# Scores in a bank pool of six, masks moved from TensorE to VectorE, and weights of two query blocks transposed in one visit

## The chip, the cores and the metric

The kernel runs on one core of one Trainium2 chip. The metric is the device time of one execution in microseconds (us). TensorE does matmuls and transposes into PSUM (eight banks of 128 partitions x 512 fp32), VectorE and ScalarE read these banks, POOL (GpSimd) works on SBUF alone, and SP (SyncE) issues most DMAs.

## The reference

One layer of a streaming encoder for 1024 prompt frames and 64 sample frames of width 1024, all in fp32:

```
h = rmsnorm(x)
q_a,k_a,v_a | q_b,k_b,v_b | f_b | gate = h @ W_in          # 8 heads of 64 in each branch, q and k normed
A: chunk-band attention: a frame reads its chunk of 64 and the 8 chunks before, bias by relative distance
B: forgetting attention: causal softmax, logit[t,s] += c[t] - c[s], c = cumsum(log sigmoid(f))
x = x + (sigmoid(gate_a) * (A @ W_pa) + sigmoid(gate_b) * (B @ W_pb)) @ W_o
x = x + HierMoE(rmsnorm(x))                                # top-1 of 4 groups, top-2 of its 8 experts
```

It returns the new x of both parts and the new key, value and forget-gate caches.

## The kernel before

**Precision.** Each fp32 operand is split into a high and a low part in the faster fp32r type; a product is two or three matmuls. So nearly every result that TensorE leaves in PSUM is read twice: ScalarE writes the rounded high part, and VectorE subtracts it from the result to get the low part.

**Stages.** First come eight passes `qkv(x)`, one for each pair of heads (four pairs of the band attention, four of the forgetting one). A pass goes through nine tiles of frames; each is a group of 24 matmuls of 384 columns (16 for the last kind of tile) into one `big` bank, which ScalarE copies to `raw` (L380). The attention of pair x runs beside the pass of pair x+1, in between its matmuls. Then come the gates, the sample frames' attention beside them, the merges with `w_pa` and `w_pb`, the output product with routing, and 32 experts, whose weights are loaded as buffers come free.

**Order.** TensorE's instructions keep the order in which the program writes them. ScalarE's, VectorE's and POOL's order is set by the compiler's own simulation as it schedules. Each `tick` in a projection (one for three matmuls) runs what is due: `at(dt, ...)` counts ticks, and `late(dt, ...)` counts `clock`, the kernel's own sum of matmul and transpose times in us. Scores of a query block come every 4.5 ticks (`PACE`). The constants are `D_W0` (8) from scores to the first part of the weights, `D_W1` (1.2) from there to the second part, `D_VAL` (4.5) to the values, and `D_TURN` (10) from the norm of q and k to their transposes.

**One head of one group.** The 1024 query frames are four groups g of two blocks j of 128. For a head and a block, `scores` multiplies q by up to 8 key blocks (5 in the band), in one or two pieces of up to 512 columns; each piece goes to a `big` bank. VectorE adds the bias and takes the row minimum (L598). In the forgetting branch VectorE has before that written bias minus c into S (L585), and TensorE adds a causal mask to the last 128 columns by a matmul of an identity with `tribig`. `softmax` takes the exponential on ScalarE (L536), the reciprocal on VectorE (L538), and scales S on ScalarE (L540). `weights` transposes S on TensorE, up to four 128x128 blocks to a `small` bank, for each block j and each part on its own; ScalarE copies the high part to `PT` (L635), and VectorE makes the low one (L636). `values` multiplies v by `PT` for both blocks.

**q and k.** `normalize` squares and sums the rows of two tiles (ScalarE L405, VectorE L408 and L410), POOL takes the power (L411) and scales the rows (L422), and `turn_qk` transposes them into another `small` bank. `stack_q` (L495) makes high and low parts of q for each group, the low ones in two buffers by turns.

**PSUM.** One pool `pp` has four `big` banks (projections, scores, gates, merges, output, experts' second products) and four `small` ones (all transposes, values, and others).

Of the kernel before, what the change touches and what calls it, by code (L numbers as in the profile page):

```python
# [24 lines left out]
CAP = 96  # L25
NOV = 22
EPS = 1e-6
NBIG, NSMALL = 4, 4
O_TURN, O_LOG, O_RANK, O_TAB = 3, 4, 7, 3
SA, SB, PTA, PTB, NORM_POOL, D_NORM, ATT0, ATT1, WPOOL, WR, SS, WO_EVERY, PF, SQ, FOX_POOL, V_POOL, RC_ACT, KT, NX, NN, NU0, E0, YB = 4, 3, 2, 1, 2, 0, 2, 26, 0, 4, 1, 3.5, 3, 2, 0, 2, 2, 1, 10, 1, 8, -1, 3  # L30
# [5 lines left out]
NW, FPAIR, D_TURN, H_NORM, H_TURN, GRP = 16, 1, 10, 0, 4, 2  # L36
D_W0, D_W1, D_VAL, PACE = 8, 1.2, 4.5, 4.5
# [9 lines left out]
class K:  # L47
    def __init__(self, tc, I, O):
        self.tc, self.nc, self.I, self.O = tc, tc.nc, I, O
        self.t, self.seq, self.due, self.later, self.clock = 0, 0, [], [], 0.0  # L50
# [136 lines left out]
    def turn_h(self, i, k0):  # L187
        nc, x, n = self.nc, self.xs[i], rows(i)
        ps = self.pp.tile([128, 4, 128], F32, name="small", bufs=NSMALL)
# [74 lines left out]
    def forget(self):  # L264
# [45 lines left out]
        def sums():  # L310
            pc = self.pp.tile([128, 2, 104], F32, name="small", bufs=NSMALL)
# [14 lines left out]
        def store():  # L326
            pn = self.pp.tile([104, 128], F32, name="small", bufs=NSMALL)
# [86 lines left out]
    def normalize2(self, br, p, i0, c, raw, T, r):  # L414
# [36 lines left out]
        self.late(D_TURN, self.turn_qk, br, p, i0, c, raw, T)  # L451

    def turn_qk(self, br, p, i0, c, raw, T):
# [3 lines left out]
        pt = self.pp.tile([128, 2, 2, 128], F32, name="small", bufs=NSMALL)  # L457
# [112 lines left out]
    def scores(self, br, p, g, h, j, T, bias, G, H):  # L570
# [13 lines left out]
        if br == 1:  # L584
            (nc.gpsimd if FOX_POOL else nc.vector).tensor_scalar(  # L585
                S[:, :n], bias[h][:, :n], self.cc[:, i, 2 * p + h:2 * p + h + 1], None, op0=OP.subtract)
        pcs = self.pieces(n)
        for x, (o, m) in enumerate(pcs):
            ps = self.pp.tile([128, 512], F32, name="big", bufs=NBIG)
            ks = slice(128 * kb0 + o, 128 * kb0 + o + m)  # L590
            qs = slice(128 * j, 128 * j + 128)
            last = br == 1 and x == len(pcs) - 1
# [10 lines left out]
        self.late(D_W0, self.weights, br, p, g, h, j, T, G, H, 0)  # L603

    def weights(self, br, p, g, h, j, T, G, H, u):

        nc = self.nc
        b0, nb = self.blocks(br, g)
        i = 2 * g + j
        kb0 = max(0, i - 4) if br == 0 else 0  # L610
        if u == 0:
            if nb > 4:
                self.late(D_W1, self.weights, br, p, g, h, j, T, G, H, 1)
        if j == 1 and u == (nb > 4):
            self.late(D_VAL, self.values, br, p, g, h, T, G, H)
        if ("PT", u) not in H:
            m, bufs = (2, self.pt_bufs) if u == 1 and nb == 6 else (4, 2)
            PT = H["PT", u] = self.ap_.tile([128, 2, m, 256], F32R, name=f"PT{m}", bufs=bufs)
            for b, jj in ((2 * g + 1, 0), (b0, 1)) if br == 0 and g >= 2 else ((2 * g + 1, 0),):
                uu, r = divmod(b - b0, 4)  # L620
                if uu == u:
                    nc.gpsimd.memset(PT[:, :, r, 128 * jj:128 * jj + 128].bitcast(F32), 0.0)
        PT = H["PT", u]
        r0, r1 = kb0 - b0, i - b0
        a, b = max(r0, 4 * u), min(r1, 4 * u + 3)
        if a > b:
            return
        S = H["S", j]
        pt = self.pp.tile([128, 4, 128], F32, name="small", bufs=NSMALL)
        for r in range(a, b + 1):  # L630
            c = (r - r0) * 128
            self.tr(pt[:, r - 4 * u, :], S[:, c:c + 128], self.ident)
        sr = slice(a - 4 * u, b + 1 - 4 * u)
        hi = PT[:, 0, sr, 128 * j:128 * j + 128]
        nc.scalar.copy(hi, pt[:, sr, :])  # L635
        nc.vector.tensor_tensor(PT[:, 1, sr, 128 * j:128 * j + 128], pt[:, sr, :], hi.bitcast(F32), op=OP.subtract)  # L636

    def values(self, br, p, g, h, T, G, H):
# [4 lines left out]
        po = self.pp.tile([128, 256], F32, name="small", bufs=NSMALL)  # L643
        for r in range(nb):
            u, rr = divmod(r, 4)
            for hl in range(2):
                self.mm(po, T["v"][(b0 + r) // 4][:, (b0 + r) % 4, h, :], H["PT", u][:, hl, rr, :],
# [23 lines left out]
    def sample2(self, br, p, P, rk, rv, qk, qh, ql):  # L671
        nc, I = self.nc, self.I
        pt = self.pp.tile([128, 4, 128], F32, name="small", bufs=NSMALL)
# [7 lines left out]
        def head(h):  # L681
# [15 lines left out]
            if br == 1:  # L697
                nc.vector.tensor_scalar(S, bias[:, :576], self.cc[:64, 12, hd:hd + 1], None, op0=OP.subtract)
            for x, o in enumerate((0, 288)):
                ps = self.pp.tile([128, 512], F32, name="big", bufs=NBIG)  # L700
                sl = slice(o, o + 288)
                last = br == 1 and x == 1
                self.mm(ps[:64, :288], qh[:, h], ks[h][:, sl], start=True, stop=False)
                self.mm(ps[:64, :288], ql[:, h], ks[h][:, sl], start=False, stop=not last)
                if last:
                    self.mm(ps[:64, 224:288], self.identb[:64, :64], self.tribig[:64, :64],
                                     start=False, stop=True)
# [7 lines left out]
        def weights(h, V, S):  # L715
            pt = self.pp.tile([128, 5, 64], F32, name="small", bufs=NSMALL)
# [11 lines left out]
        def values(h, V, PT):  # L728
            rw = slice(64 * h, 64 * h + 64)
            po = self.pp.tile([128, 256], F32, name="small", bufs=NSMALL)  # L730
# [125 lines left out]
    def out(self, m0):  # L856
# [9 lines left out]
        self.ptab = self.pp.tile([CAP, 3, 32], F32, name="ptab", tag="big", bufs=NBIG)  # L866
# [33 lines left out]
    def out_tile(self, i, mh, ml):  # L900
# [5 lines left out]
        def turn(k0):  # L906
            pt = self.pp.tile([128, 4, 128], F32, name="small", bufs=NSMALL)
# [29 lines left out]
        def logits():  # L937
            pl = self.pp.tile([128, 40], F32, name="small", bufs=NSMALL)
# [68 lines left out]
    def place(self, i, n, OH, E):  # L1007
# [3 lines left out]
        pp = self.pp.tile([128, 32], F32, name="small", bufs=NSMALL)  # L1011
# [59 lines left out]
    def turn(self, xg):  # L1071
# [3 lines left out]
        for k0 in (0, 4):  # L1075
            pt = self.pp.tile([128, 4, CAP], F32, name="small", bufs=NSMALL)
# [5 lines left out]
    def hidden(self, u, xT):  # L1082
        nc = self.nc
        ph = self.pp.tile([128, 2, CAP], F32, name="small", bufs=NSMALL)
# [74 lines left out]
    def overflow(self):  # L1159
# [8 lines left out]
        pc = self.pp.tile([128, 32], F32, name="small", bufs=NSMALL)  # L1168
# [70 lines left out]
    def run(self):  # L1239
# [24 lines left out]
        self.pp = self.open("pp", 1, PSUM)  # L1264
        pairs = [(br, p) for br in range(2) for p in range(4)]
# [152 lines left out]
```

## Time and profile before

| | |
|---|---|
| median of 3 runs | 1245.71 us (1242.77 to 1245.74) |
| profiled execution: its time, its span | 1241.81 us, 1240.0 us |
| busy in the span: TensorE, its weight loads | 96%, 89% |
| VectorE, ScalarE, POOL | 64%, 60%, 25% |
| granted TensorE clock, mean | 0.985 |

A group of instructions in the profile stands as line, engine, operation, output<-inputs by the program's names, shape and count, then its busy time and the mean duration of one in ns, then the idle time of its engine just before it with what ended that. PE is TensorE's matmuls (transposes among them), PEld its weight loads, DVE is VectorE and ACT is ScalarE. Matmuls are pipelined: the start of one to the start of the next tells what it costs, and the duration shown is longer.

### The profile page before, as it was taken

How to read it: one execution, taken by the hardware profiler on the slowest of the kernel's cores; microseconds unless marked ns; L12 is line 12 of the kernel's file. 1: busy time of each engine (PE TensorE's matmuls, PEld its weight loads, DVE VectorE, ACT ScalarE, POOL GpSimd, SP SyncE). 2: the span in 40 equal slices, each digit the busy share in tenths (PEclk: the TensorE clock that was granted, in tenths of full speed). 3: DMA queues.
4: the chain of work that ended last, by engine and by line, in shares of the span. 5: the costliest groups of instructions: out<-in, count | busy, mean ns of one | idle time of the engine just before them, and what ended most of it. 6: DMA issues, size and time to landing. Idle time of an engine off the chain costs nothing. (4 is left out here: it accounts for less than half of the span.)

```text
span 1240.0 us, 22375 instructions
## 1 busy us (share of the span) xinstructions
PE 1190.5 (96%) x7677; PEld 1105.5 (89%) x7677; DVE 788.6 (64%) x2412; ACT 740.9 (60%) x1730; POOL 314.9 (25%) x469
## 2 busy tenths in 40 slices
PE   8999999999999999999999999999999989999993
PEld 6999999999889999899899889999988859999983
DVE  5667776767388887967467686318644444666543
ACT  5789998989498898988566443423233322333331
POOL 2643435352433434100000000000000013445421
PEclk9999999999999999999999999999999998999988
DMA  8112121222322131411233332214584458999995
GB/s 283 50 61 80 44 73 52 71 65 71 69 66 73 53 84 35 81 53 32 73 92 116 104 91 75 88 33 132 199 292 161 159 195 251 302 288 285 287 290 137
DMA packets 102538, 156.31 MB, mean 126 GB/s; under 512 B 13581, under 2 KB 77941, under 8 KB 102389
## 3 DMA queue, kind: packets, MB, share of 16 engines
q1 hardware_dynamic: 92789, 124.43, 32.6%
q0 software_dynamic: 7168, 21.50, 8.1%
q10 hardware_dynamic: 2464, 8.91, 1.9%
q8 instruction: 61, 1.00, 0.3%
q14 instruction: 56, 0.46, 0.1%
HBM read 122.08 MB, written 38.23 MB: 129 GB/s over the span
## 5 line engine op out<-in xcount | busy, mean ns | idle before, releaser
L83 PE MATMUL big<-w,hTh 128*128 128x384 f32 (+1 forms) x1152 | 324.3, 354 | 1.6 <-ACT hTh L193 0.7
L83 PEld LDWEIGHTS big<-w,hTh 128*128 128x128 f32 x1152 | 204.6, 189 | 6.2 <-DVE w L234 1.0
L83 PE MATMUL big<-hTh,w 128*128 128x384 f32 (+1 forms) x768 | 205.7, 336 | 0.0
L83 PE MATMUL big<-w,hTl 128*128 128x384 f32 (+1 forms) x512 | 173.6, 339 | 0.9 <-DVE hTl L194 0.9
L83 PEld LDWEIGHTS big<-hTh,w 128*128 128x128 f32 x768 | 138.6, 189 | 1.2
L83 PE MATMUL big<-hTl,w 128*128 128x384 f32 (+1 forms) x384 | 126.4, 329 | 0.0
L636 DVE TENSOR_TENSOR PT<-small,PT 128x512 fp32r<-128x512 f32 (+2 forms) x192 | 98.9, 520 | 21.1 <-ACT PT L635 19.2
L536 ACT ACTIVATE S<-S,mns 128x640 f32<-128x640 f32 (+7 forms) x128 | 94.3, 737 | 26.3 <-DVE mns L598 25.3
L83 PE MATMUL big<-ath,w 128*128 128x384 f32 (+1 forms) x384 | 99.4, 335 | 0.0
L540 ACT ACTIVATE S<-S,rc 128x640 f32<-128x640 f32 (+7 forms) x128 | 94.0, 736 | 7.8 <-DVE rc L538 6.9
L83 PEld LDWEIGHTS big<-w,hTl 128*128 128x128 f32 x512 | 97.0, 190 | 1.3 <-DVE hTl L194 1.2
L95 PE MATMUL small<-ident,S 128*128 128x128 f32 x528 | 89.3, 273 | 4.7 <-ACT S L540 2.6
L635 ACT CAST PT<-small 128x512 fp32r<-128x512 f32 (+2 forms) x192 | 85.1, 448 | 11.3 <-PE small L95 6.7
L83 PE MATMUL small<-PT,v 128*128 128x256 f32 x608 | 83.5, 283 | 0.0
L411 POOL TENSOR_TENSOR ssr<-ssa,mhalf 128x8 f32<-128x8 f32 (+1 forms) x40 | 61.2, 1531 | 72.6 <-DVE ssa L410 55.9
L83 PEld LDWEIGHTS small<-PT,v 128*128 128x128 f32 x608 | 79.3, 188 | 0.1
L83 PE MATMUL big<-wo,mh 128*128 128x512 f32 x288 | 75.9, 402 | 0.0
L95 PEld LDWEIGHTS small<-ident,S 128*128 128x128 f32 x528 | 65.0, 140 | 10.2 <-ACT S L540 3.8
L83 PEld LDWEIGHTS big<-hTl,w 128*128 128x128 f32 x384 | 72.9, 190 | 0.0
L83 PEld LDWEIGHTS big<-ath,w 128*128 128x128 f32 x384 | 69.0, 190 | 1.4
L83 PE MATMUL big<-k,qh 128*128 128x320 f32 (+3 forms) x192 | 64.4, 339 | 3.2 <-DVE mns L598 3.2
L449 POOL TENSOR_TENSOR v<-raw,v 128x128 fp32r<-128x128 f32 x64 | 31.2, 487 | 133.3 <-DVE v L448 125.9
(259 smaller groups left out, 2568.9 us busy)
## 6 DMA issues: line engine op xcount, KB each, us to landing
uo<-in_w SPq DMA_DIRECT2D x43, 512.0 KB
ux<-in_w SPq DMA_DIRECT2D x30, 512.0 KB
ur<-in_w SPq DMA_DIRECT2D x23, 512.0 KB
wraw<-in_w_pair SPq DMA_DIRECT2D x56, 192.0 KB
wraw<-in_w_in SPq DMA_DIRECT2D x32, 192.0 KB
atd<-at SPq DMA_DIRECT2D x32, 128.0 KB
bias<-ccd SPq DMA_DIRECT2D x8, 512.0 KB
y<-in_x_prompt SPq DMA_DIRECT2D x8, 512.0 KB
```

The source lines that it names most:

```text
L83: self.nc.tensor.matmul(out, a, b, start=start, stop=stop)
L95: self.nc.tensor.transpose(out, a, ident)
L411: nc.gpsimd.tensor_tensor(r[:n, :4 * c], a[:n, :4 * c], self.mhalf[:n, :4 * c], op=OP.pow)
L449: (nc.gpsimd if V_POOL & 2 else nc.vector).tensor_tensor(V[:, i, :, 64:128], src, V[:, i, :, 0:64].bitcast(F32), op=OP.subtract)
L536: nc.scalar.activation(S[:nq, :n], S[:nq, :n], AF.Exp, bias=mn[:nq], scale=-1.0, accum_out=sm[:nq])
L540: nc.scalar.activation(S[:nq, :n], S[:nq, :n], AF.Copy, scale=rc[:nq])
L635: nc.scalar.copy(hi, pt[:, sr, :])
L636: nc.vector.tensor_tensor(PT[:, 1, sr, 128 * j:128 * j + 128], pt[:, sr, :], hi.bitcast(F32), op=OP.subtract)
```

## The change

- The banks: two `big` ones for projections and all that came after them, six `small` ones in a pool of their own, `ps`. The scores of prompt and samples go to `small`. Ahead of the output product `ps` is closed and opened again with one bank for the table of places and five `small` ones.
- The mask matmuls go, in prompt and samples. In place of the one L585 over n columns VectorE does n - 128 columns as before, and the last 128 in a scalar_tensor_tensor that subtracts c and adds `tribig`.
- `RC_ACT` 2 to 1: S of block j = 1 is scaled on VectorE, that of j = 0 still on ScalarE.
- `weights` runs once for a head and group, 7 units of `clock` after the scores of j = 1, and does all pieces of both blocks in a row; five blocks are cut 3 + 2 and six 3 + 3, where they were cut at four. `PT` is one tile for all key blocks: two buffers in the band, one in the forgetting branch.
- The transposes of q and k are put on a list 5 units after their norm begins. The next `weights` does all that stands there at its end; what has not been done 9 units after the norm began is done then.
- S has four buffers in the forgetting branch, not three, and the low part of q there one, not two.

The diff at its core:

```
-NBIG, NSMALL = 4, 4
+NBIG, NSMALL = 2, 6
-SA, SB, ..., FOX_POOL, V_POOL, RC_ACT, ... = 4, 3, ..., 0, 2, 2, ...
+SA, SB, ..., V_POOL, RC_ACT, ... = 4, 4, ..., 2, 1, ...
-NW, FPAIR, D_TURN, H_NORM, H_TURN, GRP = 16, 1, 10, 0, 4, 2
-D_W0, D_W1, D_VAL, PACE = 8, 1.2, 4.5, 4.5
+NW, FPAIR, D_TURN, D_TURN2, H_NORM, H_TURN, GRP = 16, 1, 5, 9, 0, 4, 2
+D_W0, D_VAL, PACE = 7, 4.5, 4.5
...
+    def turned_tile(self, k):
+
+        return self.ps_.tile([128, 4, 128], F32, name="small", bufs=NSMALL)[:, :k]
...
-        self.late(D_TURN, self.turn_qk, br, p, i0, c, raw, T)
+        x = [self.turn_qk, br, p, i0, c, raw, T]
+        self.late(D_TURN, lambda: self.turns.append(x))
+        self.late(D_TURN2, self.turn_now, x)
+
+    def turn_now(self, *which):
+
+        for x in which or tuple(self.turns):
+            if any(x is y for y in self.turns):
+                self.turns = [y for y in self.turns if y is not x]
+                x[0](*x[1:])
...
-        self.q_lows(self.ap_, 256, 2)
+        self.q_lows(self.ap_, 256, 2 - br)
...
-            (nc.gpsimd if FOX_POOL else nc.vector).tensor_scalar(
-                S[:, :n], bias[h][:, :n], self.cc[:, i, 2 * p + h:2 * p + h + 1], None, op0=OP.subtract)
+            c = self.cc[:, i, 2 * p + h:2 * p + h + 1]
+            if i:
+                nc.vector.tensor_scalar(S[:, :n - 128], bias[h][:, :n - 128], c, None, op0=OP.subtract)
+            nc.vector.scalar_tensor_tensor(S[:, n - 128:n], bias[h][:, n - 128:n], c, self.tribig,
+                                           op0=OP.subtract, op1=OP.add)
...
-            ps = self.pp.tile([128, 512], F32, name="big", bufs=NBIG)
+            ps = self.ps_.tile([128, 512], F32, name="small", bufs=NSMALL)
...
-            self.mm(ps[:, :m], ql[:, h, qs], K[:, ks], start=False, stop=not last)
-            if last:
-                self.mm(ps[:, m - 128:m], self.identb, self.tribig, start=False, stop=True)
+            self.mm(ps[:, :m], ql[:, h, qs], K[:, ks], start=False, stop=True)
...
-        self.late(D_W0, self.weights, br, p, g, h, j, T, G, H, 0)
+        if j == 1:
+            self.late(D_W0, self.weights, br, p, g, h, T, G, H)
...
+        self.late(D_VAL, self.values, br, p, g, h, T, G, H)
+        PT = H["PT"] = self.ap_.tile([128, 2, self.wide // 128 + 1 - br, 256], F32R, name="PT", bufs=self.pt_bufs)
+        for b, jj in ((2 * g + 1, 0), (b0, 1)) if br == 0 and g >= 2 else ((2 * g + 1, 0),):
+            nc.gpsimd.memset(PT[:, :, b - b0, 128 * jj:128 * jj + 128].bitcast(F32), 0.0)
+        for j in range(2):
+            i = 2 * g + j
+            kb0 = max(0, i - 4) if br == 0 else 0
+            r0, n = kb0 - b0, i + 1 - kb0
+            S = H["S", j]
+            m = -(-n // -(-n // 4))
+            for a in range(0, n, m):
+                b = min(a + m, n)
+                pt = self.turned_tile(b - a)
+                for r in range(a, b):
+                    self.tr(pt[:, r - a, :], S[:, 128 * r:128 * r + 128], self.ident)
+                hi, lo = (PT[:, x, r0 + a:r0 + b, 128 * j:128 * j + 128] for x in range(2))
+                nc.scalar.copy(hi, pt)
+                nc.vector.tensor_tensor(lo, pt, hi.bitcast(F32), op=OP.subtract)
+        self.turn_now()
```

## Rows read from the trace of the kernel before

**Rows 1.** The page, part 1: busy us, share of the span, instructions.
```profile
PE 1190.5 (96%) x7677; PEld 1105.5 (89%) x7677; DVE 788.6 (64%) x2412; ACT 740.9 (60%) x1730; POOL 314.9 (25%) x469
```

**Rows 2.** Busy time by stretch: us, engines in order, PEclk, DMA share, GB/s.
```profile
310.00:392.00 82.00, 77.24 (x490) 70.84 (x488) 58.12 (x165) 61.97 (x143) 34.35 (x55) 1.00 0.30 73
```

**Rows 3.** Waits of PE, 60 to 610: total us, times, longest.
```profile
PE big L83 <- DVE mns L598: 3.2, 4, 1.8
PE small L95 <- ACT S L540: 2.6, 3, 1.8
```

**Rows 4.** Timeline of PE, 411 to 416: start, us, instruction, count.
```profile
411.10 0.27 PE L95 MATMUL small<-ident,S 128*128 128x128 f32 x1
411.13 0.42 PE L83 MATMUL big<-w,hTh 128*128 128x384 f32 x1
411.39 0.34 PE L83 MATMUL big<-w,hTl 128*128 128x384 f32 x1
...
411.75 0.60 PE L95 MATMUL small<-ident,raw 128*128 128x128 f32 x4
412.11 0.78 PE L83 MATMUL big<-w,hTh 128*128 128x384 f32 x3
...
415.70 0.23 PE L83 MATMUL big<-tribig,identb 128*128 128x128 bf16 x1
415.74 1.48 PE L83 MATMUL big<-w,hTh 128*128 128x384 f32 x7
```

**Rows 5.** Groups of DVE by form, 60 to 610: busy us, mean ns.
```profile
L213 DVE SCALAR_TENSOR_TENSOR w<-wraw,small,w 128x128 fp32r<-128x128 f32 x62 | 19.0, 347 | 4.0 <-ACT w L212 3.7
...
L585 DVE TENSOR_SCALAR S<-bias,cc 128x1024 f32<-128x1024 f32 x8 | 6.2, 769 | 0.4 <-PE small L95 0.4
...
L585 DVE TENSOR_SCALAR S<-bias,cc 128x768 f32<-128x768 f32 x8 | 4.9, 613 | 0.9 <-PE small L95 0.9
```

**Rows 6.** By stretch: third, fourth groups of the first three forgetting pairs; 391.90: second pair's first two.
```profile
351.60:371.70 20.10, 18.36 (x121) 16.56 (x120) 19.06 (x54) 19.76 (x47) 5.49 (x9) 1.00 0.29 88
371.70:391.90 20.20, 19.92 (x130) 18.02 (x128) 18.14 (x48) 18.85 (x37) 9.76 (x15) 1.00 0.35 91
391.90:421.30 29.40, 29.40 (x198) 27.93 (x198) 20.43 (x61) 23.50 (x58) 10.67 (x18) 1.00 0.11 31
421.30:440.10 18.80, 17.78 (x119) 16.74 (x118) 18.15 (x52) 18.21 (x42) 4.13 (x7) 1.00 0.39 115
440.10:459.70 19.60, 19.60 (x130) 17.93 (x129) 16.69 (x45) 17.97 (x36) 9.53 (x15) 1.00 0.33 62
488.90:509.40 20.50, 18.29 (x120) 16.95 (x119) 19.20 (x64) 20.00 (x53) 3.84 (x8) 1.00 0.29 87
509.40:528.20 18.80, 18.80 (x131) 17.50 (x130) 17.15 (x47) 18.45 (x41) 5.26 (x8) 1.00 0.45 67
```

**Rows 7.** Timeline around the forgetting attention's start.
```profile
321.23 0.34 SPq L652 DMA_DIRECT2D atd<-at  x1
321.61 1.11 SPq L527 DMA_DIRECT2D bias<-ccd  x2
...
330.45 0.55 DVE L585 TENSOR_SCALAR S<-bias,cc 128x128 f32<-128x128 f32 x2 [4.40 <-DMA bias<-ccd]
```

**Rows 8.** Timeline: POOL scales q and k, TensorE transposes them.
```profile
193.75 1.19 POOL L422 TENSOR_TENSOR raw<-raw,ssr 128x256 f32<-128x256 f32 x2
...
195.45 0.60 PE L95 MATMUL small<-ident,raw 128*128 128x128 f32 x4
...
443.71 1.66 POOL L422 TENSOR_TENSOR raw<-raw,ssr 128x256 f32<-128x256 f32 x2
...
446.85 0.61 PE L95 MATMUL small<-ident,raw 128*128 128x128 f32 x4
```

**Rows 9.** Timeline in the second merge.
```profile
869.86 0.31 PE L83 MATMUL big<-atl,w 128*128 128x320 f32 x1
...
870.15 0.55 DVE L775 SCALAR_TENSOR_TENSOR z<-z,big 128x384 f32<-128x384 f32 x1
```

More of the change, by code (lines that the diff above doesn't have):

```diff
@@ L49, in __init__ @@
         self.tc, self.nc, self.I, self.O = tc, tc.nc, I, O
+        self.turns = []
         self.t, self.seq, self.due, self.later, self.clock = 0, 0, [], [], 0.0
@@ L188, in turn_h @@
         nc, x, n = self.nc, self.xs[i], rows(i)
-        ps = self.pp.tile([128, 4, 128], F32, name="small", bufs=NSMALL)
+        ps = self.turned_tile(4)
         for k in range(4):
@@ L310, in sums @@
         def sums():
-            pc = self.pp.tile([128, 2, 104], F32, name="small", bufs=NSMALL)
+            pc = self.turned_tile(2)[:, :, :104]
             lff = lf.rearrange("p i h -> p (i h)")
@@ L326, in store @@
         def store():
-            pn = self.pp.tile([104, 128], F32, name="small", bufs=NSMALL)
+            pn = self.turned_tile(1)[:104, 0]
             self.tr(pn, ccf, self.ident)
@@ L602, in scores, with weights @@
         self.softmax(mns[:, x:x + 1], S, n, 128, j < RC_ACT)
-        self.late(D_W0, self.weights, br, p, g, h, j, T, G, H, 0)
-    def weights(self, br, p, g, h, j, T, G, H, u):
+        if j == 1:
+            self.late(D_W0, self.weights, br, p, g, h, T, G, H)
+    def weights(self, br, p, g, h, T, G, H):
         nc = self.nc
         b0, nb = self.blocks(br, g)
[L609 to L636, printed above, removed]
@@ L672, in sample2 @@
         nc, I = self.nc, self.I
[L673 removed]
+        pt = self.ps_.tile([128, 4, 128], F32, name="small", bufs=NSMALL)
         for i in range(4):
@@ L697, in head @@
             if br == 1:
-                nc.vector.tensor_scalar(S, bias[:, :576], self.cc[:64, 12, hd:hd + 1], None, op0=OP.subtract)
+                c = self.cc[:64, 12, hd:hd + 1]
+                nc.vector.tensor_scalar(S[:, :512], bias[:, :512], c, None, op0=OP.subtract)
+                nc.vector.scalar_tensor_tensor(S[:, 512:], bias[:, 512:576], c, self.tribig[:64, :64],
+                                               op0=OP.subtract, op1=OP.add)
             for x, o in enumerate((0, 288)):
-                ps = self.pp.tile([128, 512], F32, name="big", bufs=NBIG)
+                ps = self.ps_.tile([128, 512], F32, name="small", bufs=NSMALL)
                 sl = slice(o, o + 288)
-                last = br == 1 and x == 1
                 self.mm(ps[:64, :288], qh[:, h], ks[h][:, sl], start=True, stop=False)
[L704 to L707, printed above, removed]
+                self.mm(ps[:64, :288], ql[:, h], ks[h][:, sl], start=False, stop=True)
                 add = bias[:, sl] if br == 0 else S[:, sl]
@@ L865, in out @@
         self.free = deque("x" * NX)
-        self.ptab = self.pp.tile([CAP, 3, 32], F32, name="ptab", tag="big", bufs=NBIG)
+        self.close("ps")
+        self.ps_ = self.open("ps", 1, PSUM)
+        self.ptab = self.ps_.tile([CAP, 3, 32], F32, name="ptab", bufs=1)
         self.next_e, self.ew, self.which = 0, [], []
@@ L937, in logits @@
         def logits():
-            pl = self.pp.tile([128, 40], F32, name="small", bufs=NSMALL)
+            pl = self.ps_.tile([128, 40], F32, name="small", bufs=NSMALL - 1)
             for k in range(8):
@@ L1010, in place @@
         V = nc.vector
-        pp = self.pp.tile([128, 32], F32, name="small", bufs=NSMALL)
+        pp = self.ps_.tile([128, 32], F32, name="small", bufs=NSMALL - 1)
         for j in range(2):
@@ L1083, in hidden @@
         nc = self.nc
-        ph = self.pp.tile([128, 2, CAP], F32, name="small", bufs=NSMALL)
+        ph = self.ps_.tile([128, 2, CAP], F32, name="small", bufs=NSMALL - 1)
         for j in range(2):
@@ L1167, in overflow @@
         self.placed = None
-        pc = self.pp.tile([128, 32], F32, name="small", bufs=NSMALL)
+        pc = self.ps_.tile([128, 32], F32, name="small", bufs=NSMALL - 1)
         for j in range(2):
```

19 lines of the change are left out of this document (9 added, 10 removed).

## The prediction, made before the result was known

> **What bounds the kernel now.** I began with the page's shares of the span: TensorE is busy for 96% of it [rows 1], so the first question is whether a matmul goes, or a wait of TensorE. The table by stretches shows where its waits lie: in the 82 us around the start of the forgetting attention TensorE is busy for 77.24 us, at a granted clock of 1.00, and the slow clock is no part of this story [rows 2]. The list of waits adds what ended them: 3.2 us for the row minimum of line 598 and 2.6 us for the scaled weights of line 540, the two largest of some 10 us between 60 and 610 us [rows 3]. So in the eight pairs of heads TensorE's own instructions set the time, save in a few places where VectorE or ScalarE comes late. Behind them gates, merges, the output product and the experts follow in TensorE's written order; a microsecond won or lost in the pairs moves all of that, the experts' weight loads too, since these start as buffers come free. The sum therefore holds terms of the pairs and few others.
>
> **Gathering the transposes.** In the timeline of TensorE, the matmul behind one transpose starts 0.03 us after it, and takes 0.42 us in place of the 0.34 of the matmul after it: 0.11 us in all. Four in a row start at 411.75 and the next matmul at 412.11, with the same lengthening behind it: 0.36 + 0.08 = 0.44 us, again 0.11 each [rows 4]. So a visit to the transposes costs nothing beyond its transposes, and gathering five visits into one gains 0 us. The bound on either side is the reading error of such a row, 0.01 us on some 100 visits: 1 us.
>
> **The masks.** 64 matmuls against `tribig` in the prompt and 8 in the samples go. The one at 415.70 lets the projections start after 0.04 us; seven of these then take 1.48 us, where 0.34 + 6 x 0.175 = 1.39 would be usual, so 0.13 us in all [rows 4]. I take 0.10, since some of the lengthening would stand behind the scores alone as well; bounds 0.04 and 0.13. All 72 are worth 7.2 us (2.9 to 9.4). By the Trainium skill (TensorE: Matmul & The Clock Gate, Back-to-back issue gap) a stream of 128-column matmuls runs at about 81 ns each; that estimate would make it 72 x 0.081 = 5.8 us.
>
> **What VectorE takes over.** Two things come to it. The j = 1 half of the scalings, which the trace shows on ScalarE only: as a tensor_scalar from SBUF to SBUF it is like line 585, 0.613 us at 768 columns and 0.769 at 1024. And the mask: line 585 gets 128 columns shorter, (0.769 - 0.613) / 2 = 0.08 us, and a scalar_tensor_tensor of 128 columns is added, like line 213 with 0.347 us: +0.27 us [rows 5]. A forgetting group of queries has two heads and two blocks. Its third group gains 2 x 0.613 + 4 x 0.27 = 2.31 us, its fourth 2 x 0.769 + 4 x 0.27 = 2.62 us.
>
> Is there room? In the table by groups, VectorE idles in the third groups of the first three pairs for 1.04, 0.65 and 1.30 us, in the fourth for 2.06, 2.91 and 1.65 [rows 6]. What doesn't fit: 1.27 + 1.66 + 1.01 in the third, 0.56 + 0 + 0.97 in the fourth, 5.5 us in all, and I take that as added time. It can be 0, if the backlog runs on into the emptier first groups, or 3 x (2.31 + 2.62) = 14.8 us, if none of the idle can be used since VectorE waits there for ScalarE. With these six groups bound by VectorE, the 24 masks in them save nothing: 48 x 0.10 = 4.8 us are left of the 7.2. In first and second groups, busy for 20.43 of 29.40 us in the second pair [rows 6], the added work costs 0, and so I count it for the fourth pair, which has no next pair's weights to split, and for the band attention, whose VectorE is in none of the larger waits; if that cover went, 32 scalings of the band at some 0.6 us would be 19 us, and I hold that for out of reach.
>
> **ScalarE's relief** is 64 scalings. It holds no one up but in the 2.6 us of [rows 3]: gain 1.5 us, bounds 0 and 2.6.
>
> **The start of the forgetting attention.** The bias load at 321.61 us is issued behind the last store of the band attention, and VectorE begins line 585 at 330.45 after 4.40 us of idle [rows 7]. The last weights come 8 + 1.2 units after their scores now, 7 then; a unit is a microsecond of the kernel's own count (0.160 us for a 384-column matmul, which takes about 0.18 by [rows 4]), so all behind them, the load too, comes 2.2 x 1.1 = 2.4 us sooner. TensorE loses 4.8 us in that stretch [rows 2]; I take 2.4 us back, bounds 0 and 4.8. The scores no longer share banks with the projections there.
>
> **q and k turned earlier.** Now 10 units after the norm begins, then at the end of a visit between 5 and 9, or at 9. The row that is turned must be normalized by POOL first. For the last tiles of a pair that ends at 445.37, and the transposes start at 446.85, 1.5 us later; in the band attention 194.94 and 195.45, 0.5 us [rows 8]. One unit earlier eats the second slack and most of the first. A visit that falls at 5 to 6 units, 4.5 x 1.1 = 5 us sooner, would leave TensorE waiting 3.5 us or more; behind it wait all projections. ScalarE's relief shortens the same chain, whose first steps are its copy and square. I take +1.5 us; bounds 0 and 9 (six pairs at 1.5).
>
> **Values behind larger visits.** They still come 4.5 units after the visit begins, but four pieces, up to 15 transposes of 0.11 us, are now inside that time, and ScalarE's and VectorE's copies of the pieces come at once. I take +1.0, bounds 0 and 4 (eight visits with 15 transposes, at 0.5 us).
>
> **One low part of q** is left in the forgetting attention. The next group's must wait till the last scores of this one are done, and the next scores come 4.5 ticks, 13.5 matmuls or some 2.4 us, later; two VectorE instructions, by line 213 some 0.4 us each (an estimate), must fit in, and TensorE's scores and projections are queued behind them. Cost 0; bound 5 (twelve changes of group at 0.4 us). The fourth S buffer can only take waits away. POOL's zeroing of the one PT tile waits for the values before, which come some 3 us ahead of the next visit: 0.
>
> **Two banks for the projections.** In the pairs and gates a group of 24 matmuls lasts 4.2 us and the copy behind it is done sooner, cost 0. In the second merge a group has 12 matmuls, 2.1 us, and VectorE lags: the third group of an output column starts about 869.7, while VectorE takes the first one's result from 870.15 to 870.70 [rows 9]. With two banks it must wait, 1.0 us; the lag doesn't add up from group to group, as TensorE's wait lets VectorE catch up. +0.7, bounds 0 and 1.5. The experts keep the order of their loads; cost 0.
>
> **Sum**, against the profiled execution's 1241.81 us: -4.8 +5.5 -1.5 -2.4 +1.5 +1.0 +0.7 = 0.0 us, 1241.8. The profiled execution lies 3.9 us under the median of the runs shown, 1245.71; moved there, 1245.7. What a measurement of this kernel can tell from no change is about 0.3%, 3.7 us.
>
> **Rivals.**
> 1. *The cover holds* (faster). VectorE's backlog is carried into the emptier first groups, and the turns and values find their data ready: -7.2 - 1.5 - 2.4 + 0.7 = -10.4, 1235.3 us. For it: the first two groups of the next pair, on which the full ones border, leave VectorE 9 us idle [rows 6]. Against it: the queue of TensorE is in order, so a late score stops the projections behind it.
> 2. *VectorE becomes the bound of the forgetting attention* (slower). Mechanism: third and fourth groups of the first three pairs; price: all 14.8 us as added time, since VectorE's idle there is waiting that no reordering fills: -4.8 + 14.8 - 1.5 - 2.4 + 1.5 + 1.0 + 0.7 = +9.3, 1255.0 us. It decides from where VectorE's added work in a group exceeds its idle in it, which is so in five of the six. The Trainium skill (Perfetto Trace Analysis, Optimization Strategy) says that a gap repeating on the engine that should be saturated can mean too few buffers. As a mechanism of this kernel: scores, turned weights and values now go round six banks, some ten per head, and each is held till VectorE has read it; if VectorE lags, TensorE waits for a bank. No run here shows that, and the time would be that of this rival.
> 3. *The turns come too early* (slower): 9 in place of 1.5 in the sum: +7.5, 1253.2 us. For it, the 0.5 us of slack in [rows 8]; against it, ScalarE's relief in just this chain.
> 4. *The turns keep their own time*: few visits fall between 5 and 9 units, so the q and k are turned alone, one unit earlier. The change then doesn't do what it says; as visits cost nothing, the time is that of the forecast.
>
> **Chances.** Forecast with rival 4: 0.36. Rival 1: 0.33. Rivals 2 and 3: 0.20 and 0.11. The forecast's own range is 1242 to 1249. For 8 in 10 the range must reach to the first two rivals: 1233 to 1257. Faster by over 0.3%: 0.33; within it: 0.36; slower: 0.31.
>
> **What would show it.** Right: the `tribig` matmuls gone and no shorter visits otherwise; VectorE over 97% in third groups of the first three pairs, with TensorE's waits there of some 2 us a pair; line 585's first start after the band's last store some 2.4 us sooner; ScalarE under 90% in these groups. Wrong: TensorE without waits from 390 to 530 us (rival 1), waits for line 598 or the weights' copies of over 10 us in sum there (rival 2), waits of the turns for POOL's normalized rows in most pairs (rival 3). A change of the stretches behind 620 us by over 3 us would mean that I missed a part.

## The result, and the profile after

The changed kernel takes 1257.23 us (median of 4 runs, 1252.58 to 1258.61) where the kernel before took 1244.24 in the runs beside it: a ratio of 1.0101, with a 95% interval of 1.0066 to 1.0136. It is slower. The forecast was no change, and the time lies 0.2 us above the range.

Its profiled execution has a span of 1256.0 us, 16.0 more than before. Line numbers move: L422 is now L427, L585 is L601 with the mask in L602, L598 is L612, L540 is L554 on ScalarE and L556 on VectorE, L636 is L641, L380 is L385; matmuls stand in L84 (before L83), transposes in L100 (before L95). The two profiled executions lie further apart than the medians (16.2 us, not 13.0). First the page's busy times of the kernel after, against [rows 1].

```profile
PE 1186.8 (94%) x7605; PEld 1110.0 (88%) x7605; DVE 828.4 (66%) x2540; ACT 697.3 (56%) x1666; POOL 313.2 (25%) x467
```

TensorE has 72 instructions and 3.7 us of work fewer, and yet the span grew: the loss is time in which TensorE does nothing. The next view lists what TensorE waited for in the kernel after, 60 to 630 us (total us, times, longest), the counterpart of [rows 3].

```profile
PE small L100 <- POOL raw L427: 10.7, 14, 2.4
PE small L100 <- DVE S L556: 3.1, 3, 1.7
PE small L84 <- DVE PT L641: 2.5, 6, 0.7
PE big L84 <- ACT raw L385: 2.4, 1, 2.4
PE small L84 <- DVE mns L612: 1.4, 2, 0.7
```

The largest line is new: the transposes of q and k wait for POOL's scaled rows. Its 14 waits belong to 7 of the 40 turns: a turn of two tiles waits once for each tile's product. In the timeline of the kernel after (start, us, engine, what; in brackets the idle time before and what ended it) one such wait stands first, and then the start of the forgetting attention.

```profile
128.45 1.67 POOL L416 TENSOR_TENSOR ssr<-ssa,mhalf 128x8 f32<-128x8 f32 x1 [1.78 <-DVE v L453]
...
130.08 0.46 POOL L454 TENSOR_TENSOR v<-raw,v 128x128 fp32r<-128x128 f32 x1
...
130.49 1.19 POOL L427 TENSOR_TENSOR raw<-raw,ssr 128x256 f32<-128x256 f32 x2
...
131.17 0.33 PE L100 MATMUL small<-ident,raw 128*128 128x128 f32 x1 [2.44 <-POOL raw L427]
...
131.74 0.90 PE L100 MATMUL small<-ident,raw 128*128 128x128 f32 x3 [0.24 <-POOL raw L427]
...
329.52 0.34 SPq L657 DMA_DIRECT2D atd<-at  x1
...
329.95 1.10 SPq L541 DMA_DIRECT2D bias<-ccd  x2
...
338.82 0.35 DVE L602 SCALAR_TENSOR_TENSOR S<-bias,cc,tribig 128x128 f32<-128x128 f32 x1 [8.04 <-DMA bias<-ccd]
...
342.39 0.35 DVE L602 SCALAR_TENSOR_TENSOR S<-bias,cc,tribig 128x128 f32<-128x128 f32 x1 [2.42 <-DMA bias<-ccd]
...
343.12 0.15 DVE L552 RECIPROCAL rc<-sm 128x1 f32<-128x1 f32 x1
...
343.31 0.40 ACT L554 ACTIVATE S<-S,rc 128x128 f32<-128x128 f32 x1 [2.81 <-DVE rc L552]
...
344.15 0.46 ACT L385 COPY raw<-big 128x384 f32<-128x384 f32 x1
...
344.66 0.45 PE L84 MATMUL big<-w,hTh 128*128 128x384 f32 x1 [2.44 <-ACT raw L385]
```

Up to 131.17 the transposes stand in TensorE's queue while POOL still does the power (1.67 us), a part of the values and the first of two products (1.19 us for both); everything behind them on TensorE waits 2.44 us, and 0.24 more for the second product. At 344.66 a chain of queues served in order ends in a bank: the reciprocal on VectorE stands behind line 602, which waits for the second head's bias; ScalarE's scaling stands behind the reciprocal; and behind the scaling stands the copy that would free one of two `big` banks.

Stretches of the kernel after (us; busy us and count of PE, PEld, DVE, ACT, POOL; granted clock, DMA share, GB/s): around four waits of TensorE, and then the third groups of the first three forgetting pairs, as in [rows 6].

```profile
129.00:132.00 3.00, 0.59 (x2) 0.40 (x3) 2.31 (x10) 2.72 (x6) 3.00 (x5) 0.92 0.09 30
132.00:136.00 4.00, 4.00 (x18) 4.00 (x18) 2.62 (x10) 2.74 (x5) 0.51 (x2) 0.63 0.24 42
136.00:140.00 4.00, 4.00 (x31) 3.97 (x30) 1.08 (x4) 1.90 (x7) 0.32 (x1) 1.00 0.00 0
...
199.30:203.00 3.70, 3.70 (x26) 3.70 (x26) 1.43 (x5) 1.63 (x5) 0.00 (x0) 1.00 0.12 35
...
262.80:266.00 3.20, 3.20 (x22) 3.20 (x21) 1.43 (x5) 1.56 (x5) 0.00 (x0) 1.00 0.15 44
...
350.40:354.00 3.60, 3.60 (x14) 3.60 (x14) 3.25 (x12) 2.05 (x7) 0.35 (x1) 0.59 0.13 41
...
363.80:379.80 16.00, 14.29 (x94) 13.40 (x93) 15.78 (x42) 13.13 (x29) 2.87 (x6) 1.00 0.33 94
...
433.40:449.90 16.50, 13.29 (x85) 11.91 (x84) 16.08 (x43) 12.85 (x28) 4.08 (x7) 1.00 0.33 93
...
502.70:519.30 16.60, 12.49 (x78) 11.12 (x77) 16.40 (x53) 14.66 (x42) 2.85 (x6) 1.00 0.28 82
```

By the starts of the passes, in the two traces, the kernel after is 0.2 us late when pass 0 begins, 10.7 when pass 6 begins and 13.9 when the second gate begins; from the output product to the end it loses 1.4 more. Passes 2 to 5 (counted from 0; the band attention runs beside passes 1 to 4 and ends in pass 5) are longer by 4.0, 1.3, 2.3 and 2.5 us. How far such differences can be trusted is shown by two traces of one kernel, the masks alone on two chips (below): passes 1 to 7 last the same in both within 0.2 us, but pass 0 differs by 2.8 us, and over all the traces here the experts last between 213 and 222 us.

### The profile page after: what moved, and what is told of

The parts are those of the page before. It is cut to its first block, busy times and chain, and to the rows that moved or that the text cites. A ratio compares the mean times of both kernels' runs of the same rounds, so it can differ in the third digit from the quotient of the medians.

```text
span 1256.0 us, 22298 instructions
## 1 busy us (share of the span) xinstructions
PE 1186.8 (94%) x7605; PEld 1110.0 (88%) x7605; DVE 828.4 (66%) x2540; ACT 697.3 (56%) x1666; POOL 313.2 (25%) x467
## 4 chain that ended last, share of the span: by engine, by line
PE 66%; DMA 11%; DVE 11%; ACT 4%; issue 4%; POOL 2%; SPq 1%; ACTq 0%; DVEq 0%; POOLq 0%
PE big L84 43%; PE small L84 16%; PE small L100 7%; DMA uo<-in_w 3%; DMA ux<-in_w 2%; DMA ur<-in_w 2%; DVE S L612 1%; DVE PT L641 1%; DVE S L601 1%; DMA bias<-ccd 1%; POOL raw L427 1%; DMA y<-hxd,ti 1%; DVE S L602 1%; ACT w L232 1%; DVE w L239 1%
## 5 line engine op out<-in xcount | busy, mean ns | idle before, releaser
L84 PE MATMUL big<-w,hTh 128*128 128x384 f32 (+1 forms) x1152 | 311.9, 346 | 5.5 <-ACT raw L385 2.4
L84 PEld LDWEIGHTS big<-w,hTh 128*128 128x128 f32 x1152 | 207.5, 190 | 9.3 <-ACT raw L385 2.7
L84 PE MATMUL big<-hTh,w 128*128 128x384 f32 (+1 forms) x768 | 202.1, 333 | 0.0
L84 PE MATMUL big<-w,hTl 128*128 128x384 f32 (+1 forms) x512 | 173.5, 339 | 0.3 <-DVE hTl L199 0.3
L84 PEld LDWEIGHTS big<-hTh,w 128*128 128x128 f32 x768 | 138.3, 189 | 1.6 <-issue 0.2
L84 PE MATMUL big<-hTl,w 128*128 128x384 f32 (+1 forms) x384 | 126.5, 329 | 0.0
L84 PE MATMUL big<-ath,w 128*128 128x384 f32 (+1 forms) x384 | 98.5, 333 | 0.4 <-DVE z L779 0.4
L84 PEld LDWEIGHTS big<-w,hTl 128*128 128x128 f32 x512 | 97.1, 190 | 0.8 <-DVE hTl L199 0.6
L641 DVE TENSOR_TENSOR PT<-small,PT 128x384 fp32r<-128x384 f32 (+2 forms) x192 | 93.1, 515 | 4.3 <-ACT PT L640 3.4
L84 PE MATMUL small<-PT,v 128*128 128x256 f32 x608 | 86.0, 285 | 5.2 <-DVE PT L641 2.5
L84 PEld LDWEIGHTS small<-PT,v 128*128 128x128 f32 x608 | 80.0, 188 | 8.6 <-DVE PT L641 5.3
L640 ACT CAST PT<-small 128x384 fp32r<-128x384 f32 (+2 forms) x192 | 76.4, 458 | 11.6 <-PE small L100 6.8
L84 PE MATMUL big<-wo,mh 128*128 128x512 f32 x288 | 75.9, 402 | 0.0
L84 PEld LDWEIGHTS big<-hTl,w 128*128 128x128 f32 x384 | 72.8, 190 | 0.2
L100 PE MATMUL small<-ident,S 128*128 128x128 f32 x528 | 69.0, 273 | 3.3 <-DVE S L556 3.1
L84 PEld LDWEIGHTS big<-ath,w 128*128 128x128 f32 x384 | 68.8, 189 | 1.9 <-DVE z L779 0.7
L100 PEld LDWEIGHTS small<-ident,S 128*128 128x128 f32 x528 | 60.9, 141 | 6.3 <-issue 3.3
L1122 POOL DMA_INDIRECT out_y<-ot,ti x32 | 54.8, 1712 | 40.9 <-DVE hl L1105 14.8
L84 PE MATMUL small<-k,qh 128*128 128x320 f32 (+3 forms) x192 | 63.4, 333 | 0.4 <-DVE ssa L415 0.3
```

Of the source, the lines that this page charges most:

```text
L84: self.nc.tensor.matmul(out, a, b, start=start, stop=stop)
L100: self.nc.tensor.transpose(out, a, ident)
L640: nc.scalar.copy(hi, pt)
L641: nc.vector.tensor_tensor(lo, pt, hi.bitcast(F32), op=OP.subtract)
L1122: return nc.gpsimd.indirect_dma_start(out=self.O["y"], out_offset=bass.IndirectOffsetOnAxis(ap=idx_r, axis=0), in_=ot[:CAP], in_offset=Non ...
```

## The experiments

All ratios are to the kernel before, run beside the kernel on the same chip. "Tick 10" in the expectations is a delay of 10 units of `clock`, GpSimd is POOL, and their third to fifth passes are passes 2 to 4 counted from 0, while the wait for the raw copy "at the start of the fifth" stands in pass 5; "the first of this set" is the gathered kernel with its turns at 10 and all scalings on ScalarE. The steps between the changed kernel and the one before are taken up one after the other.

**The turns of q and k.** The changed kernel with the turns back at 10, and the kernel before with its turns moved from 10 to 7:

```
-... D_TURN, D_TURN2, ... = ... 5, 9, ...      # after
+... D_TURN, D_TURN2, ... = ... 10, 10, ...
-... D_TURN, ... = ... 10, ...                 # before
+... D_TURN, ... = ... 7, ...
```

> The changed kernel, with q and k turned alone 10 units after their norm begins, as in the kernel before (both limits 10 in place of 5 and 9); all else of the change stays. If the early turns are the cause, the waits of the turns for POOL's scaled rows (9.9 us in the eight passes, and the slow clock behind the longest) go, and the time falls by 9 to 14 us against the changed kernel: a ratio to the kernel before of 0.998 to 1.004. If VectorE's added work is the cause, the waits move to the weights and values, and at most 4 us are won: ratio 1.007 or more.

> The kernel before, with q and k turned 7 units after their norm begins in place of 10, and nothing else. If the early turns are the cause, this alone makes the kernel slower: the slack of the last tiles of a pass (0.5 to 1.5 us) is gone, each pass waits some 2 to 3 us for POOL's rows, ratio 1.010 to 1.018. If the turns are a symptom of a VectorE that is late in the changed kernel, little happens: ratio under 1.004.

Measured: 1.0019 (0.9999 to 1.0040) and 1.0121 (1.0093 to 1.0148). Turning at 10 takes back 0.82%, some 10 us, and none of its 40 turns waits for POOL; turning at 7 alone makes the kernel before slower by 15 us. Waits of TensorE in the kernel before with its turns at 7, 59 to 630 us:

```profile
PE small L95 <- POOL raw L422: 11.1, 13, 2.5
PE small L95 <- ACT S L540: 3.7, 3, 1.7
```

Is it the bundling behind a visit, or the earliness? The turns still bundled, listed at 9 and due at 11 (here and in the next runs `RC_ACT` is 2 again, so all scalings are back on ScalarE; "one of four" and "one scaling in two on ScalarE" in the expectations mean this):

> The changed kernel with one scaling in two on ScalarE, the turns still bundled behind the next visit of the weights but not before tick 9 and at the latest at 11 (5 and 9 in the change, 1.0084; unbundled at 10, 1.0009). If only earliness costs: 0.999 to 1.003, TensorE's waits for GpSimd's product at 0 to 2 us. If the bundling itself saves: under 0.999. If the bundling itself costs: over 1.004 with few such waits.

Measured: 1.0005 (0.9986 to 1.0024), with no wait for POOL's product among TensorE's nine largest. Bundling costs and saves nothing that can be measured. The partner with the turns at 5 and 9 is this:

> The changed kernel, with both blocks' weights scaled on ScalarE as before; all else of the change stays. If VectorE's added scalings are the cause, the waits for lines of VectorE between 390 and 530 us (some 7 us) go and the ratio to the kernel before falls from 1.010 to about 1.004. If the early turns are the cause, ScalarE's load comes back into the chain ahead of them (copy, square), the waits for POOL's rows grow by 1 to 2 us in each pass, and the ratio rises to 1.012 to 1.022.

Measured: 1.0084 (1.0056 to 1.0113), which is what neither theory gave: the waits for POOL's rows fell from 10.7 us to 7.0, and the 0.17% under the changed kernel lies within the intervals. Is waiting for the product the whole of it? I first moved the product from POOL to VectorE (`NORM_POOL` 2 to 0):

> The changed kernel with its early bundled turns (5 and 9) and one scaling in two on ScalarE (1.0084), and the product that makes raw from the roots moved from GpSimd to VectorE, 72 of them, so that raw is ready earlier at the same tick. Theory A (the early turns lose by waiting for a product that ends too late): TensorE's waits for GpSimd's product, 7.0 us in ten, go, and the ratio falls to 1.000 to 1.004. Theory B (turning early loses by its place, whatever raw does: the clock, the order on TensorE or the buffers): 1.007 or more with few such waits. A price of VectorE's 72 products, if it shows, shows as waits for its casts or scalings.

Measured: 1.0086 (1.0054 to 1.0119). This didn't separate the theories: the power stayed on POOL, VectorE's product stood behind its casts, and at the three costliest turns TensorE still waited 2.23, 1.83 and 1.59 us, where it had been 2.30, 1.73 and 1.25. Waits, 59 to 630 us:

```profile
PE small L100 <- DVE raw L427: 5.6, 3, 2.2
```

So the dependence itself was taken away: the product goes to a tile of its own and the turns read the rows as ScalarE copied them. These two kernels leave the norm out of the attention's q and k, so the values behind it differ, and the experts' share of frames can differ with them.

```
-    tensor_tensor(x, x, r[...].to_broadcast([n, 4, 64]), op=OP.mult)
+    y = rn[:n, i].rearrange("t (g d) -> t g d", d=64)
+    tensor_tensor(y, x, r[...].to_broadcast([n, 4, 64]), op=OP.mult)
```

> The changed kernel with one scaling in two on ScalarE and its early bundled turns (5 and 9; 1.0084), where GpSimd writes its product beside raw and the turns read raw as it was copied: q and k of the attention stay unnormalised, and which experts the last stage picks may differ, so the stages up to the gates are compared first. Nothing is computed less, only the turns wait for the copy alone. Theory A (waiting for the product is the whole loss): the same as its partner with the turns at 10, within 0.2%, and the passes three to five of the projections back at 61 to 62 us from 63 to 66. Theory B (an early place costs by itself): 0.5% or more above its partner.

> The partner: the same product beside raw, with the turns unbundled at tick 10 (1.0009 with the product in raw). Both theories: 0.999 to 1.003, the passes three to five at 61 to 62 us.

Measured: 1.0034 (1.0017 to 1.0051) for the early turns, 1.0040 (1.0016 to 1.0063) for the late ones. With the dependence, early lost 0.75% against late (1.0084 and 1.0009); without it, nothing that can be measured, and passes 2, 3 and 4 of the early one take 63.6, 60.9 and 61.0 us, not 66.2, 63.4 and 62.9. The pair lies at 1.004, just over what was expected of the late one, which had 1.0009 with the product in place; whether that is a price of the extra tile or of the other values isn't shown. It hits both. Waits of TensorE between 59 and 365 us, with the dependence (first fence) and without it (second), both with early turns:

```profile
PE small L100 <- POOL raw L427: 7.0, 10, 2.3
PE big L84 <- ACT raw L385: 3.1, 1, 3.1
```

```profile
PE big L84 <- ACT raw L385: 2.7, 1, 2.7
PE small L84 <- DVE PT L642: 1.1, 2, 0.7
```

**The masks.** The kernel before with lines 601 and 602 of the change in place of L585 and the 72 mask matmuls; the first run is from the set of the first experiments, the second from another chip.

> The kernel before, with the mask moved from TensorE to VectorE in prompt and samples and nothing else of the change. By the prediction's price of 0.10 us a mask TensorE saves 7.2 us; with VectorE's third and fourth groups full 4.8 us or less are left: ratio 0.994 to 0.998. If VectorE is the bound there even before, the 64 x 0.27 us that it gets show as time: ratio 1.000 to 1.006.

> The masks alone once more, on another chip: 0.993 to 0.997 if 0.9946 was the kernel and not the set; over 0.998 would make the price of the banks (0.42%) smaller by as much.

Measured: 0.9946 (0.9928 to 0.9965) and 0.9939 (0.9918 to 0.9959), 1237.49 and 1236.37 us. This part of the change alone beats both kernels.

**VectorE's scalings.** `RC_ACT` = 1 added to the masks alone, and `RC_ACT` = 2 in the changed kernel with its turns at 10:

> The kernel before with the masks taken off TensorE, and one scaling in two moved to VectorE as in the change. Theory A (the added VectorE work costs it): 6 to 9 us above the masks alone, ratio 1.000 to 1.003, with waits of TensorE for VectorE's scaling or its casts of the decay's probabilities. Theory B (VectorE has room): the ratio of the masks alone, 0.994 to 0.996.

> The changed kernel with the turns of q and k back at tick 10 and one of four scalings of the probabilities back from VectorE to ScalarE. What is left of the change: masks off TensorE, gathered turns, two and six banks, one low part of q. Theory A (the added VectorE work is what the turns' lateness left unexplained): about the masks alone, 0.9946 of before, 1236 to 1239 us. Theory B (the gathered turns or the banks cost some 9 us): no better than the same kernel with the scaling on VectorE, 1.002, 1245 to 1248 us. Between: 1240 to 1244 us, the loss is shared.

Measured: 0.9974 (0.9961 to 0.9986), between its two theories, so 0.28% or 3.5 us over the masks alone, with intervals that still touch; and 1.0009 (0.9996 to 1.0022), 0.10% under its partner at 1.0019, which the intervals don't tell from none. Theory A falls: with the scalings back and the turns late the gathered kernel is still 0.6% behind the masks alone.

**Banks and gathering.** With that kernel and the masks alone as two corners, the other two are the gathered one with four and four banks and scores in `big`, and the ungathered one with two and six:

> As the first of this set, with the banks again four and four (turned tiles beside the scores), so the masks and the gathered turns at tick 10 alone. If gathering costs nothing: 0.993 to 0.996. If two big banks were the loss: this one is 4 us or more under the kernel with two and six banks, and the 2.9 us wait for the raw copy of q and k at the start of the fifth layer of projections is gone. If gathering itself is the loss: both stand at about 1.002.

> The kernel before with masks off TensorE and the banks two and six, scores and turned tiles in the six, visits ungathered. It closes the square with the masks alone (four and four, ungathered: 0.9946), gathered at four and four (1.0201), gathered at two and six (1.0009). If two big banks cost by themselves (the 2.8 us wait for the raw copy): 0.996 to 0.998. If six small banks also take waits away (softmax, casts): 0.991 to 0.994, the best so far. If the banks do nothing here: 0.9946.

| masks off TensorE, turns at 10, `RC_ACT` 2 | four and four | two and six |
|---|---|---|
| visits as before | 0.9946 (0.9928 to 0.9965) | 0.9988 (0.9966 to 1.0009) |
| gathered visits | 1.0201 (1.0181 to 1.0220) | 1.0009 (0.9996 to 1.0022) |

The lower row holds more than the gathering: the visit at 7 units, one low part of q, one `PT` tile and four buffers of S come with it and were not taken apart, save for the visit's time below. At four and four the lower row is 2.5% slower, 32 us, which none of the three cases of its expectation had. Its waits of TensorE, 59 to 630 us:

```profile
PE small L100 <- DVE PT L641: 17.0, 14, 3.3
PE small L100 <- DVE at L655: 5.1, 8, 0.9
```

A visit now asks for up to four `small` banks in a row, and each is free only when ScalarE and VectorE have read it; with four to go round, the transposes wait for VectorE's casts of the pieces before. Two and six banks take these waits away, but cost the ungathered kernel 0.4%. The Trainium skill (Perfetto Trace Analysis, Optimization Strategy) says that the same gap coming again on the engine that should be saturated can mean too few buffers; here the trace agrees, with 14 waits of up to 3.3 us that two more banks took away. One more `big` bank in exchange for a `small` one was tried on the gathered kernel:

> As the unbundled kernel at 1.0009, with three big banks and five small. If the third big bank only takes away the 2.8 us wait for the raw copy at the start of the fifth layer's projections: 0.998 to 0.9995. If the sixth small bank carries the gathered visits: 1.004 to 1.012, with waits for VectorE's casts (17 us in the kernel with four small banks that scores did not share).

Measured: 1.0066 (1.0043 to 1.0090). The wait for the raw copy is gone from the large lines, and more came at the other end, 59 to 630 us:

```profile
PE small L84 <- DVE mns L612: 7.7, 6, 2.3
PE small L84 <- DVE PT L641: 4.7, 9, 1.2
```

**Two misses and a limit.** In the gathered kernel at 1.0009 TensorE waits 4.8 us, in three times, for scaled probabilities (first fence, 59 to 630 us), so the visit was put one unit later (second fence):

> The changed kernel with the turns at tick 10 and one scaling in two on ScalarE, as in the set before (1.0009), and the visit of the weights one tick later, at 8 where the kernel before had it. Theory A (the gathered visit comes before ScalarE has scaled the second tile): TensorE's waits for scaled probabilities, 4.8 us in three, fall under 1.5 us and the ratio to 0.996 to 0.998. Theory B (the loss is VectorE's casts or the banks, or one low part of q): 1.000 to 1.002, the waits turn up at another releaser.

```profile
PE small L100 <- ACT S L554: 4.8, 3, 1.9
PE small L84 <- DVE PT L641: 2.6, 6, 0.8
```

```profile
PE small L84 <- DVE PT L641: 4.9, 14, 0.6
PE small L84 <- DVE mns L612: 4.0, 4, 1.6
```

Measured: 1.0014 (0.9995 to 1.0032). The waits changed hands and the time stayed: theory B. Two attempts to improve the masks alone failed too, a later start of the forgetting attention and later turns:

> The kernel before with the masks taken off TensorE, the forgetting attention's ticks moved later by four and its first bias loaded eight ticks ahead. Theory: TensorE's wait for the first bias (some 4 us for scores and sums at 325 to 331 us) goes, 2 to 4 us under the masks alone: ratio 0.991 to 0.993. Rival: the wait is taken up later by VectorE's backlog in the following pairs, ratio as the masks alone, 0.9946.

> The kernel before with masks off TensorE (0.9946) and the turns of q and k one tick later, at 11. Theory (lateness of raw is past at 10): the same, 0.993 to 0.997. Rival (raw is still a little late at 10): 1 to 2 us less, 0.992 to 0.994.

Measured: 1.0010 (0.9991 to 1.0028) and 0.9991 (0.9977 to 1.0005). Both lose what the masks won. With the later start TensorE's waits for line 598 rise from 4.0 us to 7.3; with the turns at 11 TensorE's waits for VectorE's casts of line 636 rise from 1.6 us to 4.1. Of the delays of the turns tried, 7 (in the kernel before) and 11 (in the masks alone) are both worse than 10.

## Why the prediction was wrong

By steps of the runs: masks -0.54%, banks +0.42, gathered visits +0.21, scalings on VectorE +0.10, early turns +0.82; together +1.01%, the measured change. In us of 1244: -6.7, +5.2, +2.6, +1.2, +10.2 = +12.5, where the sum had 0.0. Each step but the first is the difference of two ratios, good to 0.2 to 0.4% either way: the masks and the early turns are clear of that, the banks just, the other two are not. The split also hangs on the order of the steps, since the gathered visits cost 2.55% with four and four banks and 0.21% with two and six.

- **q and k turned earlier: the step that failed.** Its term was +1.5 us within bounds of 0 and 9; it measured 10.2. The mechanism was right and the size wrong. POOL's product later than the turn stood there, and so did the slack of 0.5 us [rows 8]; the upper bound was close, too, with six pairs at 1.5 us, for the trace after has 7 turns that wait, 10.7 us, 1.5 us each. What failed is the step from the bound to the term: 1.5 us has the size of one such wait in the whole kernel, and no row stands behind that. The listing at 5 lets a visit as early as that take a turn, and such a visit had been priced at 3.5 us or more. [rows 8] shows one turn of the band; in the trace before, the last turns of three passes, at 131.94, 195.45 and 256.75, come 0.7, 0.5 and 0.7 us behind the product, and these are the turns that wait 2.4, 1.7 and 1.8 us after. Rival 3 is what came, a little dearer than its 9, and had 0.11; the sign named for it shows in six of the eight pairs (1 to 5, and 7, counted from 0).
- **Two banks for the projections**: +0.7 with a bound of 1.5; measured +0.42%, 5 us, with the two intervals just apart; the spans of the pair below differ by half of that. The prediction priced the second merge alone. In the traces of the ungathered pair (the second run of the masks alone, and two and six banks; spans 1238.6 and 1241.2) the distance between the two is 0.6 us when pass 0 begins and 0.4 when the second merge begins, so passes, gates and first merge cost nothing, as predicted. The second merge takes 48.8 us in place of 47.7, near the predicted 0.7, though the gathered kernel at 1.0009, with two banks as well, takes 47.7. Behind the output product the pair differs by -1.9 us in that stage and the routing and by +3.1 in the experts. These are no more than such stages differ among the traces, with two banks (213 to 222 us for the experts) and with four (215 to 222); so where the 5 us lie stays open.
- **The start of the forgetting attention**: -2.4; it came out at none. The bias load is issued at 329.95, 15.5 us after the first matmul of pass 5; before it was 15.4 [rows 7]. What failed is "all behind them comes sooner": the visit did come sooner after its scores, but the last matmul of the band's scores came 1.6 us later against the pass, 1.4 us ahead of it where it was 3.0, and that ate most of the 2.2 units. With the turns at 10 the load still comes 14.6 us behind the first matmul; the early turns took the rest. TensorE's wait there went from the row minimum to the raw copy, 2.44 us at 344.66.
- **The masks**: all 72 at 0.10 us were 7.2, and 4.8 after the discount for full groups; alone they are worth 6.6 and 7.2 us by the medians (0.9946 and 0.9939), VectorE's added work included. The 0.10 fits, within some 2 us either way, and so does the prediction's other estimate, 5.8 us; the discount was not needed where VectorE has no scalings to do. Line 602 takes 375 ns where 347 were assumed [rows 5].
- **What VectorE takes over**: +5.5 with ScalarE's relief at -1.5, so +4.0; scalings and relief together measured +1.2 in the gathered kernel, +3.5 in the ungathered one. VectorE is busy for 98.6%, 97.5% and 98.8% of the three third groups, and ScalarE for 82%, 78% and 88%, both as the signs had it, and TensorE idles there for 1.7, 3.2 and 4.1 us (these stretches begin with VectorE's first instruction of a group, and so not quite as in [rows 6]); yet passes 6 and 7 as a whole are only 1.2 and 0.6 us longer than before. Rival 2 (14.8 us, VectorE as the bound) did not come, and that its 1255.0 us lies nearest to the measured time is luck.
- **Gathering and the values** had +1.0 together; measured +2.6, which the intervals don't tell from none. In the traces the gathered kernel at two and six banks is 2.3 us ahead of the second run of the masks alone over passes 0 to 5, and loses 8.3 from pass 6 to the second gate, where its visits are up to 15 transposes long.

Forecast and rivals were priced each with the other terms at their small values. The early turns and the banks are independent mishaps of one sign, and no case held both.

The groups of VectorE by form, 60 to 630 us of the kernel after (busy us, mean ns, idle before), against [rows 5]:

```profile
L602 DVE SCALAR_TENSOR_TENSOR S<-bias,cc,tribig 128x128 f32<-128x128 f32 x64 | 24.0, 375 | 10.6 <-DMA bias<-ccd 10.5
...
L556 DVE TENSOR_SCALAR S<-S,rc 128x1024 f32<-128x1024 f32 x8 | 6.2, 775 | 0.1
...
L601 DVE TENSOR_SCALAR S<-bias,cc 128x896 f32<-128x896 f32 x8 | 5.4, 674 | 0.0
```

The scaling's stand-in was right: 775 ns at 1024 columns, against the 769 of line 585.

## What to carry to other kernels

When an instruction of an in-order queue is moved earlier, find the end of the chain that feeds it, subtract, do so for every one of its kind, and add up those that fall short: here 7 of 40, 1.5 us each. A change that bundles several edits should be taken apart before it is judged; here the one good part, worth 0.5 to 0.6%, was hidden under others, of which the early turns cost 0.8%. PSUM banks given to one use are taken from another, and a visit that asks for several in a row needs them all at once.

## What the hardware showed that I had not expected

The waits of TensorE did not all cost the same. After the waits of 1.74 and 1.78 us at 197.58 and 261.01 the granted clock in the next stretch is 1.00, with 26 matmuls in 3.7 us and 22 in 3.2. The waits, by their first transposes:

```profile
197.58 0.33 PE L100 MATMUL small<-ident,raw 128*128 128x128 f32 x1 [1.74 <-POOL raw L427]
...
261.01 0.33 PE L100 MATMUL small<-ident,raw 128*128 128x128 f32 x1 [1.78 <-POOL raw L427]
...
348.75 0.33 PE L100 MATMUL small<-ident,raw 128*128 128x128 f32 x1 [1.57 <-POOL raw L427]
```

After the wait of 2.44 us at 131.17 it is 0.63 over 4 us, a mean of the two levels, 2.4 and 1.2 GHz, with 18 matmuls where the next 4 us hold 31; and after those of 2.44 and 1.57 us at 344.66 and 348.75 it is 0.59. By the clock, (1 - 0.92) x 3.0 in the stretch of the wait at 131.17 and (1 - 0.63) x 4.0 behind it, that wait cost 1.7 us more. Of the 4.0 us by which pass 2 is longer, its waits for POOL's rows are 2.7 us; with this clock that is 4.4, a little more than there is to explain. "The slow clock is no part of this story", which the prediction read from the kernel before, no longer held here.

The length of a wait alone doesn't decide it. In the kernel before the clock fell behind a wait of 1.97 us (first fence), and with the turns at 10 it stayed at 1.00 behind one of 2.88 us (second fence):

```profile
617.88 0.34 PE L83 MATMUL big<-sk,qh 128*64 128x288 f32 x1 [1.97 <-DVE sk L484]
618.00:622.00 4.00, 4.00 (x16) 3.98 (x17) 2.93 (x10) 2.79 (x9) 0.00 (x0) 0.57 0.10 22
```

```profile
334.28 0.44 PE L84 MATMUL big<-w,hTh 128*128 128x384 f32 x1 [2.88 <-ACT raw L385]
334.28:338.28 4.00, 4.00 (x24) 3.97 (x25) 3.25 (x12) 3.69 (x10) 2.11 (x2) 1.00 0.12 35
```

What else differs between these waits, the runs don't show. Over the whole execution the granted clock is 0.984, against 0.985 before, so the clock is a small part of the 13 us.
